# One convolution block with a SwiGLU FFN: the whole convolution input product in seven products, with banks continued from values that ScalarE writes, and late ada rows summed by adding DMAs

## The chip, the core and the metric

One core of a Trainium2 chip runs the kernel. The metric is the device time of one execution in microseconds (us). The engines are TensorE (PE), VectorE (DVE), ScalarE (ACT), GpSimd (POOL) and SyncE (SP); PEld is the loading of weights into PE. Each has its own list of instructions, which it runs in that order; they wait for one another by semaphores. SP issues most loads; POOL issues the stores, and DMAs that add.

## What is computed

One layer over 1024 tokens of width 1024, in fp32: a short gated convolution along the 64 columns of the token grid, then a SwiGLU FFN, each with a modulated RMSNorm ahead and a gated residual behind.

```python
sh1, sc1, g1, sh2, sc2, g2 = jnp.split(jax.nn.silu(c) @ ada_w + ada_b, 6, axis=-1)
h = rmsnorm(x, norm1_g) * (1 + sc1) + sh1
gate_b, gate_c, hv = jnp.split(h @ conv_w_in, 3, axis=-1)
u = gate_c * hv
conv = w[0] * left(u) + w[1] * u + w[2] * right(u)    # within rows of 64 tokens
x = x + g1 * ((gate_b * conv) @ conv_w_out)
h = rmsnorm(x, norm2_g) * (1 + sc2) + sh2
x = x + g2 * ((silu(h @ w_gate) * (h @ w_up)) @ w_out)
out = rmsnorm(x, final_g)
```

The six ada vectors come from one row times a 1024 x 6144 matrix: a sum over rows of weights, each multiplied by one number.

## The kernel before

Every fp32 product is done as three products of rounded parts (TERMS: high x high, high x low, low x high); a high part is a cast on ACT (split at L83, or L254), the low part a subtraction on DVE (L74). A matmul takes 128 x 128 of weights against 512 tokens and adds into one of 8 PSUM banks of 128x512.

The input product h @ conv_w_in has 24 tiles of 128 output columns (8 channel tiles ct for each of j = 0, 1, 2: gate_b, gate_c, hv). Two channel tiles, 0 and 1, are done directly: term0 (L286) runs over the k tiles as soon as each is normalised, in six banks, first for the tokens 0 to 511, later for the others (gated0 and mixed0 take the result). The other six channel tiles are nine pairs in Strassen-Winograd form, class Pair and its subclass Mix (L356): two column tiles by two token halves by two halves of k make seven products P1 to P7 of 12 matmuls each in place of eight. S1 to S4 are sums of the quarters of h, made by operands; weights() makes sums of weight quarters. A pair's products go into three banks X, Y, Z; P1, P6 and P7 are copied out by ACT (L368, L370, L373), and P2, P4, P5, P3 are finished by DVE (c11, c21, c22, c12). in_turn sets the order: products of one pair alternate with those of the one before it and with those of the next.

The ada vectors of the first norm are needed at the start and summed there by class Ada (L148 on ACT, L150 and L152 on DVE). Eight later pieces (two for g1, four for the second norm, two for g2) are loaded between Mixes and FFN products and summed by Ada too: sixteen rows per piece by DVE, or eight, in place. row() then makes high and low parts of the sum and adds over the partitions by two matmuls with a column of ones (L180), then writes a row to DRAM.

Up to the second token half, the order on SP, DVE, ACT and PE is that of the code, written by hand (in_order). Behind it a scheduler sets the order by the code's order as a priority, with tc.issue_after holding ada rows and loads back. The y stage (L670) multiplies the convolution's output by conv_w_out, one tile of 128 tokens at a time; the tiles of x1 go through residual and transposes (L643) to the FFN, which begins at 372.6 us (X_f, Y_f, Z_f at L356; zP at L1034) and fills the rest.

## Time and profile before

| | us |
|---|---|
| median of 3 runs | 1007.99 (1005.8 to 1008.48) |
| the profiled execution | 1006.5 |
| its span | 1004.7 |
| first direct products | 17.7 |
| first products of the y stage | 271.1 |
| first FFN product | 372.6 |

A page gives each engine's busy time and its share of the span, the chain of work that ended last, and groups of instructions by line, engine, operation and tile with busy time, mean duration of one and the idle time before them. In windows, each column is the busy time in a stretch. By stage, the columns being the stretch, PE, PEld, DVE, ACT and POOL busy, the granted clock of PE, the DMA share and GB/s:

```profile
0.00:25.00 25.00, 13.92 (x64) 12.14 (x65) 15.55 (x36) 18.12 (x36) 6.56 (x19) 0.87 1.01 310
75.00:271.00 196.00, 195.45 (x862) 160.00 (x861) 170.51 (x242) 79.64 (x125) 7.62 (x15) 1.00 0.48 144
372.00:1004.00 632.00, 625.26 (x2791) 518.18 (x2789) 435.45 (x630) 259.31 (x414) 47.59 (x82) 1.00 0.45 149
```

### The profile page before, as it was taken

The page shows a single profiled execution, that of the slowest core. Times are in us where ns is not written, and L with a number is a line of the kernel's source. Part 1 is how long each engine was busy: PE and PEld are TensorE (multiplying, and loading weights), DVE is VectorE, ACT ScalarE, POOL GpSimd, SP SyncE. Part 2 cuts the span into 40 slices and gives each one's busy share as a digit, 9 for nine tenths or more (in the row PEclk, how much of TensorE's full clock was granted, in tenths as well). Part 3 has the DMA queues.
Part 4 walks back from the last instruction along what each step waited for, and adds up shares of the span by engine and source line. Part 5 has one row for each costly group of instructions (what it writes and reads, how often), then busy time and mean ns, then how long its engine had stood idle before and what let it go on. Part 6 is the DMA issues. An engine that isn't in the chain of part 4 may idle for free.

```text
span 1004.7 us, 12134 instructions
## 1 busy us (share of the span) xinstructions
PE 983.9 (98%) x4428; PEld 814.1 (81%) x4428; DVE 728.0 (72%) x1087; ACT 446.8 (44%) x722; POOL 83.5 (8%) x153
## 2 busy tenths in 40 slices
PE   5999999999999999999999999999999999999997
PEld 4888888887888878888888888888888888888886
DVE  6879898887935789687666566566566745778875
ACT  7684433333525566233333333333334352534553
POOL 2010000000001110110110110110100110000000
PEclk8999999999999999999999999999999999999999
DMA  9921456343785232364432332332315954577533
GB/s 310 354 70 57 131 149 206 116 148 119 249 232 169 102 108 84 110 205 136 130 115 71 126 110 80 121 107 87 111 45 199 379 210 148 187 254 275 186 128 142
DMA packets 137388, 157.38 MB, mean 157 GB/s; under 512 B 6724, under 2 KB 100016, under 8 KB 137328
## 3 DMA queue, kind: packets, MB, share of 16 engines
q1 hardware_dynamic: 126944, 124.27, 39.4%
q0 software_dynamic: 9152, 29.16, 8.0%
q10 hardware_dynamic: 1232, 3.18, 0.8%
q8 instruction: 34, 0.56, 0.2%
q14 instruction: 26, 0.21, 0.1%
HBM read 123.80 MB, written 32.78 MB: 156 GB/s over the span
## 4 chain that ended last, share of the span: by engine, by line
PE 90%; DVE 4%; DMA 3%; issue 1%; SPq 1%; ACT 0%; POOL 0%; ACTq 0%; DVEq 0%; POOLq 0%
PE X_f L356 23%; PE zP L1034 20%; PE Z_f L356 12%; PE X_m L356 8%; PE y L670 8%; PE Y_f L356 6%; PE u L286 6%; PE Z_m L356 4%; PE Y_m L356 2%; DMA ada_w<-in_ada_w_dram 1%; DMA w0r<-in_conv_w_in_dram 1%; PE x1T L643 1%; DVE BP_f L74 1%; DMA wr_m<-in_conv_w_in_dram 1%; DVE ada_acc L152 1%
## 5 line engine op out<-in xcount | busy, mean ns | idle before, releaser
L74 DVE TENSOR_TENSOR BP_f<-wr_f,BP_f 128x512 fp32r<-128x512 f32 x154 | 104.7, 687 | 60.7 <-ACT BP_f L83 59.0
L83 ACT CAST BP_f<-wr_f 128x512 fp32r<-128x512 f32 x154 | 94.0, 621 | 84.8 <-PE Z_f L356 51.6
L1034 PE MATMUL zP<-w3l_P,a3h_P 128*128 128x512 f32 (+1 forms) x319 | 121.8, 382 | 0.0
L1034 PE MATMUL zP<-w3h_P,a3l_P 128*128 128x512 f32 (+1 forms) x319 | 121.7, 382 | 0.0
L1034 PE MATMUL zP<-w3h_P,a3h_P 128*128 128x512 f32 (+1 forms) x319 | 120.4, 382 | 0.6 <-DVE bot L80 0.6
L1034 PEld LDWEIGHTS zP<-w3h_P,a3h_P 128*128 128x128 f32 x319 | 59.9, 188 | 12.3 <-DVE bot L80 0.8
L1034 PEld LDWEIGHTS zP<-w3l_P,a3h_P 128*128 128x128 f32 x319 | 60.0, 188 | 11.7
L1034 PEld LDWEIGHTS zP<-w3h_P,a3l_P 128*128 128x128 f32 x319 | 60.0, 188 | 11.6
L74 DVE TENSOR_TENSOR a3l_P<-a3l_P,a3h_P 128x1024 fp32r<-128x1024 f32 (+1 forms) x42 | 47.4, 1135 | 26.9 <-ACT a3h_P L889 26.9
L83 ACT CAST BP_m<-wr_m 128x512 fp32r<-128x512 f32 x63 | 37.8, 622 | 58.9 <-DVE wr_m L74 31.8
L152 DVE SCALAR_TENSOR_TENSOR ada_acc<-ada_w,cols,ada_acc 128x512 f32<-128x512 f32 (+1 forms) x88 | 61.3, 709 | 1.6 <-ACT ada_acc L148 0.5
L356 PE MATMUL X_f<-A11h,BP_f 128*128 128x512 f32 x176 | 57.7, 390 | 0.0
L356 PE MATMUL X_f<-AS3h,BP_f 128*128 128x512 f32 x176 | 57.6, 389 | 0.0
L356 PE MATMUL X_f<-AS2h,BP_f 128*128 128x512 f32 x176 | 57.6, 389 | 0.0
L356 PE MATMUL X_f<-A22h,BP_f 128*128 128x512 f32 x176 | 57.6, 389 | 0.0
L356 PE MATMUL Z_f<-AS4h,BP_f 128*128 128x512 f32 x176 | 57.6, 389 | 0.0
L356 PE MATMUL Y_f<-A12h,BP_f 128*128 128x512 f32 x176 | 57.5, 389 | 0.0
L356 PE MATMUL Z_f<-AS1h,BP_f 128*128 128x512 f32 x176 | 57.4, 389 | 0.0
L74 DVE TENSOR_TENSOR BP_m<-wr_m,BP_m 128x512 fp32r<-128x512 f32 x63 | 42.3, 686 | 14.4 <-ACT BP_m L83 13.9
L670 PE MATMUL y<-woh,vh_t 128*128 128x512 f32 x128 | 50.4, 394 | 0.0
L670 PE MATMUL y<-woh,vl_t 128*128 128x512 f32 x128 | 49.9, 390 | 0.0
L670 PE MATMUL y<-wol,vh_t 128*128 128x512 f32 x128 | 49.9, 390 | 0.0
(287 smaller groups left out, 2239.3 us busy)
## 6 DMA issues: line engine op xcount, KB each, us to landing
wr_f<-in_ffn_w_in_dram SPq DMA_DIRECT2D x44, 512.0 KB, 3.9
ada_w<-in_ada_w_dram SPq DMA_DIRECT2D x64, 256.0 KB, 5.9
w_P<-in_ffn_w_out_dram SPq DMA_DIRECT2D x30, 512.0 KB, 5.6
a3l_P<-ad_S SPq DMA_DIRECT2D x20, 512.0 KB, 6.2
wr_m<-in_conv_w_in_dram SPq DMA_DIRECT2D x18, 512.0 KB, 5.5
ad<-a POOLq DMA_DIRECT2D x33, 256.0 KB, 2.6
ada_w<-in_ada_w_dram SPq DMA_DIRECT2D x16, 512.0 KB, 3.9
a3l_P<-ad SPq DMA_DIRECT2D x15, 512.0 KB, 3.7
```

Of the source, the lines that this page charges most:

```text
L74: return nc.vector.tensor_tensor(o, a, b, op=ALU.subtract)
L83: nc.scalar.copy(hi, raw)
L152: nc.vector.scalar_tensor_tensor(acc, self.rows[k], by, acc, op0=ALU.mult, op1=ALU.add)
L286: nc.tensor.matmul(ps0[ct, j, h], lhsT=w0[k][wi][:, j, ct * P:(ct + 1) * P], rhs=h_of(k, h)[hi], start=(k == 0 and i == 0), stop=(k == KD ...
L356: mm = nc.tensor.matmul(ps, lhsT=w[:, wi, 2 * kp + kk, :], rhs=A[aname, kp][hi][:, kk, :], start=(first and kp == 0 and kk == 0 and i == 0 ...
L643: nc.tensor.transpose(ps2[:, i * P:(i + 1) * P], xn[:, k * P:(k + 1) * P], ident)
L670: mm = nc.tensor.matmul(ys[t][n], lhsT=vt[t][vi][:, k, :], rhs=wo[k][wi][:, n * H:(n + 1) * H], start=(k == 0 and i == 0), stop=(k == KD - ...
L1034: mm = nc.tensor.matmul((zs[t] if to is None else to)[:, cols], lhsT=a[ai][:, k % 2, t * P:(t + 1) * P], rhs=w[wi][:, k % 2, cols], start= ...
```

## The change

All 24 column tiles are now done in seven products, as twelve pairs (PAIRS): pair (i, j) is channel tiles i and i + 4 of j. P1 and P2, which need only the first token half, are done at the start: for seven pairs (EARLY) by term0, k tile by k tile, and for five more by class First, four k tiles at a time. P1 is copied to SBUF between (save_p1, L325). The other five products are class Mixes, two pairs at a time in one bank each, in the order P5, P6, P7, P4, P3. After P5, ACT copies the bank to z5 and writes the saved P1 into the bank (L429, L430); P6 goes on adding to it, DVE takes v = bank + z5, P7 goes on; after P4, ACT writes v into the bank (L444) and P3 goes on. Direct products, class Mix and mixed0 go.

For the eight later pieces, class AdaRow loads rows as before; ACT multiplies each in place (L186); POOL's DMAs with accum_op add them (L188, L191): three of 512 KB and one of 256 KB a piece, each on the destination of the one before. In the convolution their tiles are of the pool t_s, which u, cv, xT and the operands use as well. Rows of a piece are no longer held back by issue_after. In the startup, ada pieces have one column tile for k = 0 to 3; weights come as 128x896 (before 128x768) in two DMAs. The y stage begins with three tiles of the first four k's (before two, six k's).

```diff
+    class AdaRow:
+        def __init__(self, j0, nj, d0, w, tile):
+            self.j0, self.d0, self.w = j0, d0, w
+            self.name = f"ada{j0}_{d0}"
+            for k0 in range(0, KD, 2):
+                raw = tile(f"{self.name}_w{k0}", [P, 2, nj, w])
+                for j in range(nj):
+                    nc.sync.dma_start(raw[:, :, j, :], aw[:, k0:k0 + 2, j0 + j, d0:d0 + w])
+                for i in range(2):
+                    nc.scalar.mul(raw[:, i], raw[:, i], cs[:, k0 + i:k0 + i + 1])
+                if k0:
+                    nc.gpsimd.dma_start(both, raw, accum_op=ALU.add)
+                else:
+                    both = raw
+            nc.gpsimd.dma_start(both[:, 0], both[:, 1], accum_op=ALU.add)
+            self.acc = [both[:, 0]]
...
+    PAIRS = [(0, 2), (0, 1), (1, 2), (1, 1), (0, 0), (2, 2), (2, 1), (1, 0), (3, 2), (3, 1), (2, 0), (3, 0)]
+    EARLY = PAIRS[:7]
+    place = {(i, j): 3 * j - 2 + i if j else 0 for i, j in EARLY}
...
     def load0(k):
-        w0raw[k] = t_wraw(f"w0r_{k}", [P, 3, C0 * P])
-        nc.sync.dma_start(w0raw[k], conv_w_in[k * P:(k + 1) * P, :].rearrange("p (j n) -> p j n", j=3)[:, :, :C0 * P])
+        w0raw[k] = t_wraw(f"w0r_{k}", [P, 7, P])
+        rows = conv_w_in[k * P:(k + 1) * P, :]
+        nc.sync.dma_start(w0raw[k][:, 1:, :].rearrange("p (j i) n -> p j (i n)", j=2),
+                          rows.rearrange("p (j n) -> p j n", j=3)[:, 1:, :3 * P])
+        nc.sync.dma_start(w0raw[k][:, 0, :], rows[:, :P])
...
+    def term0(k, pair, terms=range(3)):
+        if pair not in xbank:
+            xbank[pair] = bank("x%d_%d" % pair)
+        for i in terms:
+            wi, hi = TERMS[i]
+            nc.tensor.matmul(xbank[pair], lhsT=w0[k][wi][:, place[pair], :], rhs=h_of(k, 0)[hi],
+                             start=(k == 0 and i == 0), stop=(k == KD - 1 and i == 2), skip_group_check=True)
...
+    def save_p1(pair):
+        n = PAIRS.index(pair)
+        if n % 2 == 0:
+            saved[n // 2] = t_s(f"p1_{n // 2}", [P, 2, H])
+        saved[pair] = saved[n // 2][:, n % 2, :]
+        nc.scalar.copy(saved[pair], xbank[pair])
...
+    def first_done(pair):
+        (i, j), ps = pair, xbank.pop(pair)
+        if j == 2:
+            mixed[i, 0] = t_s(f"u{i}_0", [P, 2, H])
+            nc.scalar.copy(mixed[i, 0][:, 0, :], ps)
+        elif j == 1:
+            mul(mixed[i, 0][:, 0, :], ps, mixed[i, 0][:, 0, :])
+        else:
+            if i % 2 == 0:
+                gate11[-1 - i] = t4(f"gate11_{i}", [P, 2, H])
+            gate11[i] = gate11[-1 - i // 2 * 2][:, i % 2, :]
+            nc.scalar.copy(gate11[i], ps)
...
+    class First:
+        def __init__(self, pair):
+            (i, j), self.pair = pair, pair
+            self.raw = t_wraw("wf%d_%d" % pair, [P, KD, P])
+            nc.sync.dma_start(self.raw, conv_w_in[:, j * D + i * P:j * D + (i + 1) * P].rearrange("(k p) n -> p k n", p=P))
+        def weights(self, half):
+            self.w = [t_wop("wf%s%d_%d_%d" % ((s, half) + self.pair), [P, KH, P]) for s in "hl"]
+            split(*self.w, self.raw[:, half * KH:(half + 1) * KH, :])
+        def products(self, half):
+            if half == 0:
+                xbank[self.pair] = bank("x%d_%d" % self.pair)
+            for k in range(KH):
+                for i, (wi, hi) in enumerate(TERMS):
+                    nc.tensor.matmul(xbank[self.pair], lhsT=self.w[wi][:, k, :], rhs=h_of(half * KH + k, 0)[hi],
+                                     start=(half == 0 and k == 0 and i == 0), stop=(half == 1 and k == KH - 1 and i == 2),
+                                     skip_group_check=True)
+            if half == 0:
+                save_p1(self.pair)
+            else:
+                first_done(self.pair)
...
+    class Mixes:
+        def __init__(self, n):
+            self.n, self.pairs = n, PAIRS[2 * n:2 * n + 2]
+            self.raw = {}
+            for name, tile, k0 in (("11", 0, 0), ("12", 1, 0), ("22", 1, KH), ("21", 0, KH)):
+                self.raw[name] = t_wraw(f"wr{name}_{n}", [P, 2, KH, P])
+                for a, (i, j) in enumerate(self.pairs):
+                    c = j * D + (i + tile * KH) * P
+                    self.last_load = nc.sync.dma_start(
+                        self.raw[name][:, a],
+                        conv_w_in[k0 * P:(k0 + KH) * P, c:c + P].rearrange("(k p) n -> p k n", p=P)).ins
+            self.w = {}
...
+        def weights(self):
+            b11, b12, b22, b21 = [self.raw[name] for name in ("11", "12", "22", "21")]
+            sub(b11, b12, b11)
+            self.weight("P5", b11)
+            yield
+            sub(b11, b22, b11)
+            self.weight("P6", b11)
+            yield
+            sub(b12, b22, b12)
+            self.weight("P7", b12)
+            yield
+            sub(b21, b21, b11)
+            self.weight("P4", b21)
+            yield
+            self.weight("P3", b22)
+            yield
+        def weight(self, pname, raw):
+            w = self.w[pname] = [t_wop(f"B{pname}{s}_m{self.n}", [P, 2, KH, P]) for s in "hl"]
+            split(*w, raw)
...
+        PLAN = (("P5", "S1"), ("P6", "S2"), ("P7", "S3"), ("P4", "22"), ("P3", "S4"))
+        def products(self):
+            ps = [bank(f"m{self.n}_{a}") for a in range(2)]
+            z5, v = [[t2(f"{name}_{self.n}_{a}") for a in range(2)] for name in ("z5", "v")]
+            for pname, aname in self.PLAN:
+                for a, (i, j) in enumerate(self.pairs):
+                    for k in range(KH):
+                        for n, (wi, hi) in enumerate(TERMS):
+                            mm = nc.tensor.matmul(ps[a], lhsT=self.w[pname][wi][:, a, k, :],
+                                                  rhs=A[aname, k // 2][hi][:, k % 2, :],
+                                                  start=(pname == "P5" and k == 0 and n == 0),
+                                                  stop=(k == KH - 1 and n == 2), skip_group_check=pname != "P5")
+                    self.last_mm = mm.ins
+                    if pname == "P5":
+                        nc.scalar.copy(z5[a], ps[a])
+                        nc.scalar.copy(ps[a], saved[i, j])
+                        if j == 2:
+                            mixed[i, 1] = t_s(f"u{i}_1", [P, 2, H])
+                    elif pname == "P6":
+                        add(v[a], ps[a], z5[a])
+                    elif pname == "P7":
+                        to = mixed[i, 1][:, 1, :]
+                        if j == 2:
+                            add(to, ps[a], z5[a])
+                        else:
+                            add(z5[a], ps[a], z5[a])
+                            mul(to, to, z5[a])
+                    elif pname == "P4":
+                        self.put(mixed[i, 0][:, 1, :], ps[a], j)
+                        nc.scalar.copy(ps[a], v[a])
+                    else:
+                        self.put(mixed[i, 1][:, 0, :], ps[a], j)
+                        self.finish(i, j)
...
+                for m, pair in enumerate(EARLY):
+                    term0(k, pair)
+                    if k == KH - 1:
+                        save_p1(pair)
+                    if m == 2 and k == p.ks[-1]:
+                        r.total()
...
+        for n, pair in enumerate(EARLY):
+            for k in (KD - 2, KD - 1):
+                term0(k, pair)
+            if n < TH:
+                xs[n].scale()
+            elif n < TH + 2:
+                more[n - TH].weights(0)
+            first_done(pair)
         transposed(0)
-        two = [next(mix) for _ in range(2)]
-        term0(KD - 1, 0, cts=(0,))
+        more[0].products(0)
         transposed(1)
-        term0(KD - 1, 0, cts=(1,))
-        gated0(0, 0)
-        transposed(2), transposed(3)
...
+    for m in more:
+        m.weights(1)
+        m.products(1)
+    mixes = Mixes(0)
+    weights = mixes.weights()
+    next(weights)
+    for n in range(3):
+        next(ops)
+        next(weights)
+        if n == 1:
+            for kp in range(2):
+                operand("22", kp, xT[1][kp + 2])
+    next(weights)
...
-    def start_piece(p):
+    def start_piece(p, tile):
         with tc.issue_after(p.last_load):
-            a = Ada(*pieces.pop(0), itertools.repeat(t_wraw))
-        a.sums()
-        pending.append(a)
-    def between_mixes(p):
-        if pending:
-            finish_piece(p)
-        if pieces and (p.j != 2 or p.ct == C0):
-            start_piece(p)
-    in_turn(itertools.chain(two, mix), 9, between_mixes)
+            pending.append(AdaRow(*pieces.pop(0), tile))
+    for n in range(6):
+        mixes.products()
+        if n < 5:
+            mixes = Mixes(n + 1)
+            for _ in mixes.weights():
+                pass
+        while pending:
+            finish_piece()
+        for _ in range((1, 1, 2, 2, 0, 0)[n]):
+            start_piece(mixes, t_s)
...
-    K0 = KD - 2
-    for t in range(2):
+    K0, T0 = KD - 4, 3
+    for t in range(T0):
         vt[t] = v_tile(t, ((0, K0), (K0, KD)))
         y_steps(t, range(K0))
     for t in range(2):
-        vt[t + 2] = v_tile(t + 2, ((0, KD),))
+        if t == 0:
+            vt[T0] = v_tile(T0, ((0, KD),))
+        else:
+            vt[T0 + 1] = v_tile(T0 + 1, ((0, KD),))
```

On DVE, at the start of the first Mixes (m0), the changed order runs, from the u product of pair (3, 1) (the first row, u_0_877), to the first v (rows of operands S1 to S4 and of weights BP.. of m0; wr are raw weight quarters):

```order
L80 TENSOR_TENSOR u_0_877<-x_1_759,u_0_877 128x512
L74 TENSOR_TENSOR AS2l_950<-S_0_832,AS2h_949 128x1024
L74 TENSOR_TENSOR wr_0_931<-wr_0_934,wr_0_931 128x1024
L74 TENSOR_TENSOR S_1_833<-S_1_833,xT_1_98 128x1024
L74 TENSOR_TENSOR xT_1_102<-xT_1_98,xT_1_102 128x1024
L74 TENSOR_TENSOR BP5l_m_945<-wr_0_931,BP5h_m_944 128x1024
L74 TENSOR_TENSOR AS2l_955<-S_1_833,AS2h_954 128x1024
L74 TENSOR_TENSOR wr_0_931<-wr_0_937,wr_0_931 128x1024
```

After four more rows of the same kind it ends:

```order
L74 TENSOR_TENSOR A22l_979<-xT_2_103,A22h_978 128x1024
L74 TENSOR_TENSOR xT_2_99<-xT_2_99,S_0_832 128x1024
L74 TENSOR_TENSOR BP7l_m_975<-wr_0_934,BP7h_m_974 128x1024
L74 TENSOR_TENSOR A22l_983<-xT_3_104,A22h_982 128x1024
L74 TENSOR_TENSOR AS4l_988<-xT_2_99,AS4h_987 128x1024
L74 TENSOR_TENSOR xT_3_100<-xT_3_100,S_1_833 128x1024
L74 TENSOR_TENSOR wr_0_940<-wr_0_940,wr_0_931 128x1024
L77 TENSOR_TENSOR v_0_1012<-m_0_1008,z_0_0_1010 128x512
```

In the kernel before, the same operands stood here, interleaved with finishing rows of other pairs, while the direct products of the second token half ran on PE:

```order
L74 TENSOR_TENSOR AS1l_955<-S_0_951,AS1h_954 128x1024
L74 TENSOR_TENSOR S_0_951<-S_0_951,xT_0_97 128x1024
L74 TENSOR_TENSOR xT_2_99<-xT_2_99,S_0_951 128x1024
L74 TENSOR_TENSOR BP_m_2_1023<-wr_m_2_1_612,BP_m_2_1023 128x512
L74 TENSOR_TENSOR BP_m_2_1026<-wr_m_2_1_612,BP_m_2_1026 128x512
L77 TENSOR_TENSOR S_1_952<-xT_1_102,xT_3_104 128x1024
L74 TENSOR_TENSOR xT_1_102<-xT_1_98,xT_1_102 128x1024
L74 TENSOR_TENSOR AS1l_960<-S_1_952,AS1h_959 128x1024
L74 TENSOR_TENSOR AS2l_983<-S_0_951,AS2h_982 128x1024
L74 TENSOR_TENSOR S_1_952<-S_1_952,xT_1_98 128x1024
```

The sums and subtractions are the same; what stands behind them is new: v_0_1012, a drain of a product's bank, where before only rows of later products followed.

On ACT in the fifth Mixes (m4), between the drains of P5 (L429, L430), the changed order has (ada_768 is a piece for the second norm; a trailing x2 means two such rows):

```order
L186 ACTIVATE ada_512_w_1898<-ada_512_w_1898,cols 128x512 x2
L83 CAST BP3h_m_1857<-wr_4_1831 128x1024
L186 ACTIVATE ada_768_w_1905<-ada_768_w_1905,cols 128x512 x2
L186 ACTIVATE ada_768_w_1910<-ada_768_w_1910,cols 128x512 x2
L186 ACTIVATE ada_768_w_1916<-ada_768_w_1916,cols 128x512 x2
L429 COPY z_4_0_1931<-m_0_1929 128x512
L186 ACTIVATE ada_768_w_1922<-ada_768_w_1922,cols 128x512 x2
L430 COPY m_0_1929<-p_4_738 128x512
L429 COPY z_4_1_1932<-m_1_1930 128x512
L430 COPY m_1_1930<-p_4_738 128x512
```

Before, a Mix late in the convolution had (e_m and u_m are copies of a bank, BP_m a weight's high part, cv a convolution's first product):

```order
L83 CAST BP_m_0_1724<-wr_m_0_0_1642 128x512
L370 COPY e_m_1_1528<-X_m_1_1515 128x512
L83 CAST BP_m_0_1727<-wr_m_0_1_1644 128x512
L83 CAST BP_m_0_1732<-wr_m_0_1_1644 128x512
L373 COPY u_m_1_1638<-X_m_1_1515 128x512
L83 CAST BP_m_0_1735<-wr_m_0_1_1644 128x512
L368 COPY e_m_0_1665<-X_m_0_1652 128x512
L83 CAST BP_m_0_1739<-wr_m_0_0_1642 128x512
L294 ACTIVATE cv_1694<-u_1461,cols_576 128x1024
```

There, casts and copies alternated; now eight products of ada rows stand between casts and the copy and write of a bank.

On POOL the first late piece's DMAs are:

```order
L188 DMA ada_0_w_1195<-ada_0_w_1199 128x1024
L188 DMA ada_0_w_1195<-ada_0_w_1204 128x1024
L188 DMA ada_0_w_1195<-ada_0_w_1209 128x1024
L191 DMA ada_0_w_1195<-ada_0_w_1195 128x512
L205 DMA ada_0_b<-in_ada_b_dram 1x16x32
L209 DMA g_row<-ada_0_b 16x1x32
L188 DMA ada_512_w_1413<-ada_512_w_1417 128x1024
```

In their place before:

```order
L312 DMA vd<-cv_0_693 128x512
L312 DMA vd<-cv_0_732 128x512
L312 DMA vd<-cv_1_966 128x512
L312 DMA vd<-cv_1_975 128x512
L183 DMA ada_0_b<-in_ada_b_dram 1x16x32
L187 DMA g_row<-ada_0_b 16x1x32
L183 DMA ada_512_b<-in_ada_b_dram 1x16x32
```

The first four add into ada_0_w_1195, one behind the other; the row matmuls on PE (L202) wait for the last of them through a cast. Before, POOL issued only stores, and rows of ada_b.

More of the change, by code (lines that the diff above doesn't have):

```diff
@@ L253, in modulate1 @@
         nc.scalar.activation(o, o, AF.Identity, scale=scale1[:, k:k + 1], bias=shift1[:, k:k + 1])
-        nc.scalar.copy(h_of(k, h)[0], o)
+        if h == 0:
+            nc.scalar.copy(h_of(k, h)[0], o)
     def low1(k, h):
@@ L277, in low0 @@
         sub(w0[k][1], w0raw[k], f(w0[k][0]))
-    def term0(k, h, terms=range(3), cts=range(C0)):
-        for ct in cts:
-            for j in JS:
-                if k == 0 and 0 in terms:
-                    ps0[ct, j, h] = bank(f"u{ct}_{j}_{h}")
-                for i in terms:
-                    wi, hi = TERMS[i]
-                    nc.tensor.matmul(ps0[ct, j, h], lhsT=w0[k][wi][:, j, ct * P:(ct + 1) * P], rhs=h_of(k, h)[hi],
-                                     start=(k == 0 and i == 0), stop=(k == KD - 1 and i == 2))
+    def term0(k, pair, terms=range(3)):
[5 more added lines that the diff above has]
+                             start=(k == 0 and i == 0), stop=(k == KD - 1 and i == 2), skip_group_check=True)
@@ L517, in trunk_kernel @@
         for i in range(TH):
-            if i == TH - 1:
-                p.sums(3)
             xs[i].scale()
@@ L524, in trunk_kernel @@
                     xs[i].copies(g)
-        p.sums()
+            if i == TH - 2:
+                p.total()
+        xs[-1].copies(0)
         high0(0)
-        for g in range(2):
-            xs[-1].copies(g)
+        r.sums(4, 1)
+        columns(p)
+        xs[-1].copies(1)
         low0(0)
-        p.total()
-        columns(p)
         while r:
@@ L555, in trunk_kernel @@
         low1(KD - 1, 0)
-        for i in range(TH):
-            xs[i].scale()
-        mix = mixes()
+        more = [First(pair) for pair in PAIRS[7:]]
+        squares(xs)
+        cols2 = columns_of("cols2", 4 * KD, rows2)
+        g2c, cwc = cols2[:, R_G2:R_G2 + KD], cols2[:, R_CW:]
         def transposed(i):
@@ L725, in then @@
             h2_of(t - 1 if t > 2 else 0, xr[t - 1 if t > 2 else 0])
-        y_steps(t, range(KD), 6 if t == 3 else 4, then)
+        y_steps(t, range(K0 if t < T0 else 0, KD), 6 if t < 4 else 4, then)
         if t == 2:
```

162 lines of the change are left out of this document (52 added, 110 removed).

## The prediction

> **What bounds the kernel now.** I read the page first: which engine is full, and which engine the chain that ended last runs through.
>
> ```profile
> span 1004.7 us, 12134 instructions
> ...
> PE 983.9 (98%) x4428; PEld 814.1 (81%) x4428; DVE 728.0 (72%) x1087; ACT 446.8 (44%) x722; POOL 83.5 (8%) x153
> ...
> PE 90%; DVE 4%; DMA 3%; issue 1%; SPq 1%; ACT 0%; POOL 0%; ACTq 0%; DVEq 0%; POOLq 0%
> ```
>
> PE is busy 98% of the span and holds 90% of the chain. So a product that goes saves its time only as long as PE finds the next one ready. How close the other engines are is read from the stage that changes. The windows of 25 us through the convolution's products give, from the left, the busy time of PE, PEld, DVE and ACT, the granted clock and the DMA share:
>
> ```profile
> core 0: us, PE busy (x) PEld busy (x) DVE busy (x) ACT busy (x) POOL busy (x), PEclk, DMA share, GB/s
> 75.00:100.00 25.00, 25.00 (x112) 20.71 (x111) 24.76 (x30) 11.49 (x16) 0.00 (x0) 1.00 0.16 50
> 100.00:125.00 25.00, 25.00 (x112) 20.67 (x112) 20.31 (x31) 10.57 (x17) 1.59 (x3) 1.00 0.44 132
> 125.00:150.00 25.00, 25.00 (x112) 20.45 (x111) 24.02 (x36) 9.54 (x15) 0.98 (x2) 1.00 0.53 157
> 225.00:250.00 25.00, 24.45 (x108) 19.65 (x107) 18.96 (x31) 9.88 (x18) 0.52 (x1) 1.00 0.38 114
> ```
>
> PE is full in nearly every one, but DVE stands at 19.0 to 24.8 us of 25: it is a second engine just behind the bound, covered rather than idle. The waits of PE in the part of the span before the FFN say the same (what waited, for whom, us in total, times, longest):
>
> ```profile
> PE cols_ps L106 <- ACT xT L221: 7.3, 1, 7.3
> PE u L286 <- ACT A11h L254: 2.5, 1, 2.5
> PE u L286 <- DVE A11l L74: 0.7, 1, 0.7
> PE X_m L356 <- ACT u_m L373: 0.6, 1, 0.6
> ```
>
> The first three fall at the start. After them, up to the y stage, PE waits once, 0.6 us. All that this kernel can lose is therefore cover, and the question for each edit is how much cover it leaves.
>
> **What the change saves.** The chain gives the price of a product of four k tiles and three terms, and of the second token half's direct products:
>
> ```profile
> 74.12 32.67 PE u L286 x144
> 106.79 2.72 PE X_m L356 x12
> ```
>
> 12 matmuls take 2.72 us, 0.2267 each. Before, input products for channel tiles 0 and 1 are 288 matmuls and the nine Mix pairs 756, together 1044; after, twelve pairs of seven products of 12 are 1008. The 36 that go are worth 36 x 0.2267 = **8.2 us**. This is certain as busy time of PE. The ada sums that leave DVE (64 in the middle of the kernel) are worth nothing directly, since DVE is not the bound, and they come back on ACT and as DMAs.
>
> **What the change takes away: cover.** Before, a Mix spread its products over three banks, and products of one pair alternated with those of the other two; a bank was drained while PE filled others. Now the five products of a pair share one bank, two pairs alternate, and between two products of one bank stand only the 12 matmuls of the other: 2.72 us. In that time ACT or DVE has to read the bank, and after P5 and P4 ACT has to write it as well. Durations, by line and by shape, for ACT and then DVE (busy, mean ns of one, idle before and its releaser):
>
> ```profile
> L253 ACT ACTIVATE xT<-xT,shift,scale 128x512 f32<-128x512 f32 x16 | 12.6, 811 | 1.0 <-DVE shift L170 1.0
> L274 ACT CAST w0h<-w0r 128x768 fp32r<-128x768 f32 x8 | 6.8, 845 | 6.9 <-DMA w0r<-in_conv_w_in_dram 6.9
> L370 ACT COPY e_m<-X_m 128x512 f32<-128x512 f32 x9 | 5.3, 587 | 12.9 <-PE X_m L356 12.9
> L148 ACT ACTIVATE ada_acc<-ada_w,cols 128x512 f32<-128x512 f32 x4 | 2.8, 718 | 4.6 <-DMA ada_w<-in_ada_w_dram 4.6
> L254 ACT CAST A12h<-xT 128x512 fp32r<-128x512 f32 x4 | 2.5, 621 | 0.1
> L83 ACT CAST AS4h<-xT 128x1024 fp32r<-128x1024 f32 x2 | 2.1, 1055 | 0.8 <-DVE AS3l L74 0.5 <-PE u L286 0.3
> ...
> L74 DVE TENSOR_TENSOR w0l<-w0r,w0h 128x768 fp32r<-128x768 f32 x8 | 7.6, 952 | 0.5 <-ACT w0h L274 0.5
> L77 DVE TENSOR_TENSOR e_m<-Y_m,e_m 128x512 f32<-128x512 f32 x6 | 4.1, 685 | 2.9 <-PE Y_m L356 2.9
> L74 DVE TENSOR_TENSOR AS1l<-S,AS1h 128x1024 fp32r<-128x1024 f32 x2 | 2.5, 1226 | 0.0
> ```
>
> A copy out and a write in are 0.59 + 0.59 = 1.2 us, a DVE sum 0.69: each fits in 2.72 if the engine is free at that moment. What stands ahead of them in program order decides.
>
> *Start, +5 us.* At the end of k = 3 the last of seven copies of P1 sums waits for that k's last matmul; behind it, and ahead of the operand that k = 4 begins with, stand an ada product, a modulation and a cast: 0.59 + 0.72 + 0.81 + 0.62 = 2.7 us with nothing left for PE. Before, no copy from a bank stood there. At k = 5 to 6 the new scale and shift come with 12 matmuls (2.7 us) left; two modulations with casts, the high weights, the low weights and the low operand follow one another: 2 x (0.81 + 0.62) + 0.85 + 0.95 + 0.69 = 5.4, so 2.6 us are open (the weight tile is 128x896 now, which I left at the price of 128x768). Together 5.3; I take 5. Bounds: 0, if the 3.2 us that PE waits there before go in exchange and a little more, to 8.
>
> *Mix 0, +7 us.* On DVE, 18 rows of 128x1024 stand between the u product and v of the first bank. The u product waits for the third of five P2 products. From there to the end of the first P6 are five products, 60 matmuls, 13.6 us; another 2.7 us pass under the other bank's P6 before P7 needs v to be done. DVE needs 0.69 + 18 x 1.226 + 0.69 = 23.4 us, 7.1 more. Before, the same preparation had the 144 direct products of the second half as cover, 32.7 us, and DVE was busy 24.8 of 25 even then. Bounds: 4 to 9 (by how far such rows overlap, and how early DVE can run ahead).
>
> *Mix 4, +8 us.* In the ACT order the cast BP3h waits until the last P5 but one matmul is done; behind it, ahead of the write into the first bank for which P6 waits, stand six ada products, a copy and two more products: 1.06 + 8 x 0.72 + 2 x 0.59 = 8.0 us. No product is left to hide them: the other bank's P5 is over. Bounds: 7 to 14, if loads of those ada rows come late.
>
> *Mixes 1, 2, 3 and 5, +7 us.* The same cast stands ahead of the second bank's pair of copies, with one or two ada products in some: 1.06 + 0.59 + 0.59 + 0.72 = 3.0 against 2.72, and more where ACT comes to it late. I take 1 each, and 3 more in Mix 3, where ada products stand ahead of the first copy too. Bounds 0 to 12.
>
> **The adding DMAs, +30 us.** Before has none, so they are bounded by the nearest transfers of the same queue, and the loads they wait for:
>
> ```profile
> ad<-a POOLq DMA_DIRECT2D x33, 256.0 KB, 2.6
> ...
> ada_w<-in_ada_w_dram SPq DMA_DIRECT2D x16, 512.0 KB, 3.9
> ...
> x1d<-x POOLq DMA_DIRECT2D x8, 512.0 KB, 3.0
> ...
> vd<-cv POOLq DMA_DIRECT2D x6, 512.0 KB, 4.5
> ```
>
> A piece has four steps on one destination, each waiting for the one before: 3 x (3.0 to 4.5) + 2.6 = 11.6 to 16.1 us from its last ada product on. After it come the cast, the low part and two row matmuls that stand in PE's order, with PE blocked until they run. A Mix is 120 matmuls, 27.2 us. One piece in a Mix (the first two) fits; but the next Mix's u and cv tiles take the buffers of its raw rows, so DVE and ACT, too, wait for POOL: I take 3 us each. Two pieces in a Mix (twice) need 23 to 32 us of steps, a first load of 3.9 and 16 ada products of 0.72, 39 to 48 us if nothing overlaps, 12 to 20 over the 27.2. I take 12 each, the lower end, since some of it runs beside stalls counted above. 2 x 3 + 2 x 12 = 30. Bounds: 0 if all of it stays inside the Mixes, 80 if a step takes 9 us (six chains of 3 x 9 + 4.5 are 189 us, against 109 in four Mixes).
>
> The Trainium skill, "Collectives: The Full Stack", section "The bandwidth ceiling: the fold count and why AG ≠ RS ≠ AR", says that a reducing transfer runs at about half the rate of a copy, because it reads two sources through one ring. No run here shows an adding DMA yet; by that rule a step would be nearer to 9 us than to 4.5, which is a rival below.
>
> *Nothing for the rest.* In the y stage three tiles begin early instead of two; the matmuls are the same, and the products hide the new order (0 to 5 us, if the first transposes of x1 come late). In the FFN two pieces go from DVE to ACT and POOL under its products, which fill PE.
>
> **Sum.** -8.2 + 5 + 7 + 8 + 7 + 30 = +48.8 us. On the profiled execution of 1006.5 us that is 1055.3; the median of the runs lies 1.5 us above it, which makes **1057 us**.
>
> **Rivals.**
> - *The queues cost, the adding DMAs don't.* If steps of 3.0 us run beside the loads, 30 becomes 0 to 8: 1008 - 8.2 + 27 + 4 = 1031. For: DMA share is only 0.4 to 0.5 in these windows. Against: row matmuls and buffers tie PE and DVE to the last step. With all queue terms at their lower bounds (11 us) it reaches 1011.
> - *Faster: the cover holds.* In the Mix stage ACT is busy only 10 of 25 us and DVE loses the ada sums. If each bank comes back within the 2.72 us of the other one's product, PE stays full and only the 36 matmuls count: 1008.0 - 8.2 = 1000. It decides at that point alone, 2.72 us per drain, and fails where ACT's eight ada products stand in between. Against it: three of the places above go past it by rows that the order fixes.
> - *Slow sums.* With a step at 9 us the term is 80 instead of 30: 1107. For it only that a sum reads twice; against it, nothing in this trace.
>
> **Chances.** Forecast 0.60 (1038 to 1085), queues alone 0.20 (1011 to 1038), faster 0.10, slow sums 0.10 (1085 to 1130). The range 1012 to 1115 leaves out the faster case and about half of the slow one. A measurement of this kernel can tell about 0.3% (3 us) from no change: faster by more 0.10, within it 0.04 (the low edge of queues alone), slower 0.86.
>
> **What would show it.** Right: PE busy 8 us less while the span grows; PE waits in the m banks for ACT's writes, the longest in Mix 4 at some 8 us; a wait of Mix 0 for DVE's v; row matmuls of ada waiting for a cast behind POOL; an adding DMA of 512 KB landing in 3 to 6 us. Wrong: PE full in windows of the Mix stage (then the faster rival); PE waits of ACT alone, with no row matmul or POOL among releasers (queues alone). The forecast fails first if the adding DMAs land well under 3 us or over 9.

## The result, and the profile after

The changed kernel takes 1103.0 us (median of 4 runs, 1098.0 to 1106.5), the kernel before beside it 1007.2: a ratio of 1.0948, 95% interval 1.09 to 1.0996. It is 95.9 us slower, where the forecast of 1057 us stood 49.8 above the same 1007.2; the time lies inside the stated range, but outside the forecast's own 1038 to 1085, in the case of slow sums, which had a chance of 0.10. The four runs lie 8.5 us apart, and the profiled execution is the one of 1098.0. Its page (the span, busy time and share of each engine, the chain that ended last by engine):

```profile
span 1096.3 us, 12225 instructions
...
PE 1003.8 (92%) x4404; PEld 819.4 (75%) x4404; DVE 691.0 (63%) x975; ACT 500.3 (46%) x787; POOL 108.9 (10%) x183
...
PE 61%; DMA 17%; DVE 8%; issue 7%; ACT 4%; SPq 2%; POOL 1%; POOLq 0%; DVEq 0%; ACTq 0%
```

PE holds 61% of the chain, where it held 90%. Two things are to be read from the second line. PE's idle time is 1096.3 - 1003.8 = 92.5 us; before it was 1004.7 - 983.9 = 20.8, so 71.7 us more. And PE is *busy* for longer, though 36 matmuls of 128x512 are gone: 983.9 - 8.2 = 975.7 us were due, 1003.8 are there, 28.1 us more. 71.7 + 28.1 - 8.2 = 91.6 us is the whole difference of the two spans.

By stage, PE is idle 21.5 us up to the first product of the Mixes (11.8 before, up to the last direct product), 57.8 in the Mixes (0.6) and 13.2 behind them (8.5). What PE waited for in the whole span (us in total, times, longest):

```profile
PE m L423 <- ACT m L430: 15.1, 6, 8.7
PE m L423 <- DVE u L77: 14.1, 3, 6.8
PE ada_ps L202 <- ACT ada_h L83: 11.6, 3, 7.8
PE m L423 <- ACT m L444: 10.8, 3, 7.3
PE cols_ps L106 <- ACT xT L243: 6.8, 1, 6.8
PE x L317 <- ACT A11h L277: 4.6, 1, 4.6
PE m L423 <- DVE v L77: 3.7, 1, 3.7
PE X_f L507 <- ACT e_f L521: 2.9, 1, 2.9
PE x L317 <- DVE A12l L74: 2.7, 1, 2.7
PE x L317 <- ACT A12h L277: 2.6, 1, 2.6
```

Four rows, 51.6 us, stand for the Mixes: ACT's writes of p1 (L430) and v (L444), DVE's sum that drains P7 (L77), and row matmuls of ada (L202). Before, the Mixes had one wait of 0.6 us.

The busy time is read from windows (busy us of PE, PEld, DVE, ACT, POOL with the number of instructions, PE's granted clock, DMA share, GB/s), here of two stretches with a gap:

```profile
170.00:180.00 10.00, 3.22 (x9) 2.31 (x8) 2.52 (x3) 1.33 (x2) 1.11 (x2) 0.69 0.81 188
290.00:300.00 10.00, 5.02 (x12) 3.96 (x13) 1.23 (x1) 4.84 (x9) 1.85 (x3) 0.50 1.04 242
```

In the second row 12 matmuls take 5.02 us in place of 2.72: the clock is at half. Over the whole span PE works 44.2 us at a granted clock of 0.5, in ten stretches; before, 6.8 us in one, at the start. By 0.43 us a matmul against 0.227 half of that time would do at full clock, so the clock costs an estimated 22.1 us here and 3.4 before: 18.7 of the 28.1. The timeline of the Mixes shows why, and is the clearest sight of the ACT queue that the prediction read from the order (start, duration, instruction, idle time ahead of it and who ended it; ACT first, then PE):

```profile
286.75 1.03 ACT L83 CAST BP3h_m<-wr 128x1024 fp32r<-128x1024 f32 x1
287.68 3.78 ACT L186 ACTIVATE ada_w<-ada_w,cols 128x512 f32<-128x512 f32 x6
291.37 0.56 ACT L429 COPY z<-m 128x512 f32<-128x512 f32 x1
293.12 1.33 ACT L186 ACTIVATE ada_w<-ada_w,cols 128x512 f32<-128x512 f32 x2 [1.19 <-DMA ada_w<-in_ada_w_dram]
294.35 0.57 ACT L430 COPY m<-p 128x512 f32<-128x512 f32 x1
...
285.92 0.39 PE L423 MATMUL m<-AS1h,BP5l_m 128*128 128x512 f32 x1
294.98 0.79 PE L423 MATMUL m<-AS2h,BP6h_m 128*128 128x512 f32 x1 [8.67 <-ACT m L430]
295.57 0.63 PE L423 MATMUL m<-AS2l,BP6h_m 128*128 128x512 f32 x1
296.00 0.63 PE L423 MATMUL m<-AS2h,BP6l_m 128*128 128x512 f32 x1
```

This is the fifth Mixes' turn from P5 to P6. Behind the cast, six ada products, a copy, a load awaited for 1.19 us and two more products stand ahead of the write: PE is idle for 8.67 us, and starts again at 0.43 us a matmul instead of 0.227, until about 300.2. The Trainium skill, "TensorE: Matmul & The Clock Gate", section "Part 1: The HAM clock gate (the "warmup" mystery)", says that the clock falls to half after an idle window of some 3.4 us and returns after a busy one; the trace agrees at this gap, with half speed for 5.2 us. The gaps of 2.65 and 2.70 us of this trace's start, shorter than such a window, were followed by half speed too, for 3.4 us each, so a gap need not be that long; three others of 2.5 to 2.9 us, at 311, 326 and 565 us, were not.

The adding DMAs, beside transfers of the same size on POOL's queue (KB each, median us to landing):

```profile
ada_w<-ada_w POOLq DMA_DIRECT2D x24, 512.0 KB, 6.1
...
vd<-cv POOLq DMA_DIRECT2D x8, 512.0 KB, 4.3
x1d<-x POOLq DMA_DIRECT2D x8, 512.0 KB, 3.1
...
ada_w<-ada_w POOLq DMA_DIRECT2D x8, 256.0 KB, 4.8
```

A piece's chain is 3 x 6.1 + 4.8 = 23 us from its first step on. What else hangs on it is seen at the second Mixes, in DVE's timeline and PE's:

```profile
168.37 1.22 DVE L74 TENSOR_TENSOR BP6l_m<-wr,BP6h_m 128x1024 fp32r<-128x1024 f32 x1
176.65 0.69 DVE L77 TENSOR_TENSOR u<-m,z 128x512 f32<-128x512 f32 x1 [7.06 <-DMA ada_w<-ada_w]
...
177.39 0.80 PE L423 MATMUL m<-A22h,BP4h_m 128*128 128x512 f32 x1 [6.78 <-DVE u L77]
```

DVE's sum needs a tile for u; the tile is one of the piece's raw rows and is free only when the adding DMA out of it has landed. DVE stands for 7.06 us, with PE's bank undrained.

### The profile page after: what moved, and what is told of

The parts are those of the page before. It is cut to its first block, busy times and chain, and to the rows that moved or that the text cites. A ratio compares the mean times of both kernels' runs of the same rounds, so it can differ in the third digit from the quotient of the medians.

```text
span 1096.3 us, 12225 instructions
## 1 busy us (share of the span) xinstructions
PE 1003.8 (92%) x4404; PEld 819.4 (75%) x4404; DVE 691.0 (63%) x975; ACT 500.3 (46%) x787; POOL 108.9 (10%) x183
## 4 chain that ended last, share of the span: by engine, by line
PE 61%; DMA 17%; DVE 8%; issue 7%; ACT 4%; SPq 2%; POOL 1%; POOLq 0%; DVEq 0%; ACTq 0%
PE zP L1140 19%; PE X_f L507 16%; PE Z_f L507 8%; DMA ada_w<-ada_w 8%; PE y L772 6%; PE m L423 4%; PE Y_f L507 4%; DMA ada_w<-in_ada_w_dram 3%; PE x L317 1%; DVE BP_f L74 1%; DMA vl_t<-vd 1%; DMA w0r<-in_conv_w_in_dram 1%; SPq L140 1%; PE x L358 1%; ACT xT L275 1%
## 5 line engine op out<-in xcount | busy, mean ns | idle before, releaser
L186 ACT ACTIVATE ada_w<-ada_w,cols 128x512 f32<-128x512 f32 x64 | 42.8, 715 | 39.6 <-DMA ada_w<-in_ada_w_dram 38.1
L507 PE MATMUL X_f<-AS3h,BP_f 128*128 128x512 f32 x176 | 57.8, 390 | 2.9 <-ACT e_f L521 2.9
L772 PE MATMUL y<-wol,vh_t 128*128 128x512 f32 x128 | 49.8, 389 | 0.0
L995 ACT CAST a3h_P<-a3l_P 128x1024 fp32r<-128x1024 f32 (+1 forms) x42 | 40.7, 977 | 17.6 <-DMA a3l_P<-ad_S 10.9
L74 DVE TENSOR_TENSOR wr_f<-wr_f,wr_f 128x512 f32<-128x512 f32 x66 | 45.3, 690 | 4.2 <-DMA wr_f<-in_ffn_w_in_dram 2.7
```

Of the source, the lines that this page charges most:

```text
L74: return nc.vector.tensor_tensor(o, a, b, op=ALU.subtract)
L186: nc.scalar.mul(raw[:, i], raw[:, i], cs[:, k0 + i:k0 + i + 1])
L507: mm = nc.tensor.matmul(ps, lhsT=w[:, wi, 2 * kp + kk, :], rhs=A[aname, kp][hi][:, kk, :], start=(first and kp == 0 and kk == 0 and i == 0 ...
L772: mm = nc.tensor.matmul(ys[t][n], lhsT=vt[t][vi][:, k, :], rhs=wo[k][wi][:, n * H:(n + 1) * H], start=(k == 0 and i == 0), stop=(k == KD - ...
L995: nc.scalar.copy(hi, f(lo))
```

## The experiments

Theory, when they began: the time goes to ACT's and DVE's queue at the turns of the banks, to the chain of slow adding DMAs and the tiles that it holds, and a part of each gap again to the lowered clock. Rival 1: the shared bank by itself. Rival 2: the adding DMAs alone, whatever the cover. Runs without a range are single ones, each beside the kernel before at 1007.4 to 1007.6 us. "Bare" is the changed kernel with the late pieces cut to two rows; the pieces' vectors are then not the reference's, as in the runs without adds.

**No adds.** In class AdaRow (in before's form of it too, further down):

```diff
-                if k0:
-                    nc.gpsimd.dma_start(both, raw, accum_op=ALU.add)
-                else:
+                if k0 == 0:
                     both = raw
-            nc.gpsimd.dma_start(both[:, 0], both[:, 1], accum_op=ALU.add)
```

> The changed kernel without the adding DMAs (the rows of the late pieces other than the first are loaded and multiplied, but not added). Theory: the chains of adding DMAs and what is tied to them (row matmuls of ada, the tiles that u and cv take over) cost some 35 us of PE's idle time and some 12 us more by the lowered clock after gaps, so 1055 us (1045 to 1070), with the waits of PE at the ada rows under 3 us and ACT's ada products still ahead of the bank writes of the fifth Mixes (8 us). Rival 1 (the shared bank itself: two pairs, one bank each): 1085 or more. Rival 2 (the adding DMAs are all of it): 1020 or less.

1062.4 us: 40.6 less. PE's waits now (the same lines stand three numbers lower):

```profile
PE m L420 <- ACT m L427: 17.6, 6, 9.7
...
PE ada_ps L199 <- ACT ada_h L83: 3.9, 2, 2.5
PE m L420 <- ACT m L441: 3.0, 3, 1.7
```

The waits for u are gone, the waits for the row matmuls fell from 11.6 to 3.9 and those for v's write from 10.8 to 3.0; the writes of p1, behind ada products, are as late as ever. So the adding DMAs cost 41 us by the medians, or 36 by the spans of the two profiles; three waits that hang on their tiles fell by 30 us, and PE's busy time by 6. Both rivals are out of their ranges.

**Bare.** `range(0, KD, 2)` becomes `range(0, 2, 2)` in AdaRow, without the adds.

> The changed kernel with the late pieces cut to their first two rows (loads, products and adds of the others left out). Theory: the 8 us wait behind ada products in the fifth Mixes goes as well, and what stays is the start (6 us), Mix 0 (7 us) and some casts ahead of bank copies: 1030 us (1020 to 1042). Rival 1 (the shared bank): 1075 or more. Rival 2 (adding DMAs alone): the same as without the adds, within 4 us.

1035.2 us: another 27.2 less; the wait for L427 falls from 17.6 to 3.2. That is what ACT's products and the loads they wait for cost, with the lowered clock behind the gaps (PE loses 6.2 us by it, 17.9 without the adds). Still 27.8 us more than the kernel before, which sums its pieces besides.

**DVE sums.** The late pieces by class Ada as before (`a = Ada(*pieces.pop(0), itertools.repeat(tile)); a.sums()`), in the change's places and with AdaRow's row(). A first form without that row() could not be built and has no time; 1045 us (1030 to 1060) had been expected of it.

> The changed kernel, with the late pieces summed by DVE as before, from the same tiles (nothing left out). Theory (what costs is a chain of slow adding DMAs that holds tiles, and ACT's ada products behind loads that wait for these tiles): no chain, no ada products on ACT, 12 us of DVE per piece instead; in the Mixes with two pieces DVE is over-full: 1050 us (1038 to 1062), with PE's waits for DVE's v and u. Rival 1 (the shared bank): 1080 or more. Rival 2 (adding DMAs alone, no cost of the place of the sums): 1036 or less, as without pieces.

1061.4 us, at the upper end. PE's wait for DVE's v rose to 13.7 us. It gains as much as leaving out the adds, with the whole computation done: the chain was dearer than the sums. But the sums aren't free either, 26 us over the bare kernel.

**Before with the adding DMAs.** AdaRow put into the kernel before, called by its start_piece.

> The kernel before, with its late pieces summed by ACT's products and the adding DMAs in place of DVE (nothing left out). Theory: with three banks a pair and one piece in a Mix the cover hides most of it; row matmuls of ada wait a little: 1013 us (1006 to 1025). Rival 1: 1007, within 3. Rival 2 (the adding DMAs cost by themselves, whatever the cover): 1045 or more.

1057.5 us, +50: the theory fell here, and the time lies in rival 2's range. I had put the loss down to the cover that the change takes away; the kernel with its full cover loses as much. Its waits, SP's wait ahead of the loads of ada rows (L199), and ACT's idle time ahead of the ada products (the last row: busy, mean ns, idle before and its releaser):

```profile
PE X_m L378 <- ACT e_m L392: 21.0, 6, 7.7
PE X_m L378 <- ACT u_m L395: 10.9, 3, 6.8
...
SPq L199 <- DMA ada_w<-ada_w: 86.9, 12, 11.1
...
L201 ACT ACTIVATE ada_w<-ada_w,cols 128x512 f32<-128x512 f32 x64 | 43.7, 717 | 75.1 <-DMA ada_w<-in_ada_w_dram 72.2 <-DVE sa L77 2.7
```

ACT stands 72 us for loads of ada rows, ahead of the copies for which PE waits: a load needs a tile that an adding DMA still holds, and SP waits 86.9 us for such tiles. That the adds merely slow the loads down is not what the trace shows: a load lands 5.8 us after its issue here, 5.5 in the next run, which has no adds. One thing differs from the change besides cover: the rows lie in the pool of raw weights here, which has 5 buffers, not in t_s with its 32. Whether the kernel before would lose as much with more buffers wasn't tried.

**Before with ACT's products, no adds.** The edit of the first experiment in that kernel.

> The kernel before with ACT's ada products, but without the adding DMAs (rows of the late pieces other than the first are loaded and multiplied, not added; with the adds it took 1057.5 us). Theory: what costs is that a tile is held until its adding DMA has landed, so that the next rows load late and ACT's products, which wait for the loads, stand ahead of the bank copies. Without adds the tiles come free at once: 1015 us (1007 to 1025). Rival (ACT's products are in the way by themselves): 1040 or more.

```profile
L201 ACT ACTIVATE ada_w<-ada_w,cols 128x512 f32<-128x512 f32 x64 | 44.0, 719 | 28.6 <-DMA ada_w<-in_ada_w_dram 27.0 <-DVE BP_f L74 1.4
```

1011.2 us. The same products in ACT's queue cost next to nothing here, though DVE has lost its sums; the adds, by the tiles they hold, cost 46, and ACT's wait for the loads falls from 72 to 27 us. So cover hides ACT's products (in the changed kernel they and their loads cost 27) but, with these buffers, not the chain (46 with the cover, 41 without).

**Two banks a pair.** P1's sum is written into the bank of P6, P7 and P4 ahead of time, P5 has its own, and v is written into that for P3:

```diff
-            ps = [bank(f"m{self.n}_{a}") for a in range(2)]
+            xs, zs = [[bank(f"{name}{self.n}_{a}") for a in range(2)] for name in "mz"]
...
+            for a, pair in enumerate(self.pairs):
+                nc.scalar.copy(xs[a], saved[pair])
...
+                    ps = (zs if pname in ("P5", "P3") else xs)[a]
...
                     elif pname == "P6":
-                        add(v[a], ps[a], z5[a])
+                        add(v[a], ps, z5[a])
+                        nc.scalar.copy(zs[a], v[a])
```

In this form no matmul has begun the bank of P6 when ACT writes to it; so the adding-on of P1's sums is not that of the reference, while the instructions timed are the same.

> The changed kernel with two banks for a pair: P1's sum is written into the bank of P6, P7, P4 ahead of time, P5 has a bank of its own, and v is written into that for P3; no product waits for a write by ACT right after it (nothing left out, adding DMAs as in the change). Theory: PE's waits for these writes (25.9 us) go, but ACT still stands behind loads that wait for adding DMAs, and z5 and the u copies come late in their place: 1085 us (1070 to 1098). Rival 1 (the shared bank is the cost): 1065 or less. Rival 3 (the wait only changes its name): 1099 to 1105.

> The changed kernel with the late pieces cut to their first two rows (1035.2 us so) and two banks for a pair. Theory: without ada products ahead, ACT's writes cost PE only 5.4 us, and these go: 1029 us (1026 to 1032). Rival 1 (the shared bank is the cost also without pieces): 1015 or less. Rival 3 (no gain, drains by DVE are late instead): 1034 or more.

1095.7 us with the adding DMAs, 1030.6 bare: 7.3 and 4.6 less. With the adds the waits move from ACT's writes to DVE's sums:

```profile
PE m L426 <- DVE z L77: 16.3, 3, 9.6
PE m L426 <- DVE v L77: 12.6, 4, 6.7
PE m L426 <- DVE u L77: 8.6, 2, 6.4
```

So the shared bank is worth some 5 us by the bare kernels, single runs both; 7.3 is less than the four runs of the change lie apart. Rival 1 is out.

**The start, bare.** The last three copies of P1 stand behind the first operand of k = 4; k = 6 of all pairs ahead of k = 7; the low operand of k = 6 ahead of the low weights of k = 7 (`low1(KD - 2, 0)` above `low0(KD - 1)`).

> The changed kernel with the late pieces cut to their first two rows (1035.2 us so), and in the start the last three copies of P1 behind the first operand of k = 4, the k = 6 products of all seven pairs ahead of those of k = 7, and the low operand of k = 6 ahead of the low weights of k = 7. Theory: the waits of 2.6 and 2.7 us go: 1030 us (1028 to 1033). Rival (Mix 0 is held by DVE anyway, so the time is lost there instead): 1034 to 1036.

1034.0 us, 1.3 less: the rival's time. The 2.6 us wait is down to 0.6 and that of 2.7 us to 1.2, and the first Mixes start 5.5 us earlier (106.7 against 112.2 us), but the last product of the Mixes comes only 1.2 earlier (296.3 against 297.5). The waits of the first Mixes are as long as they were, so the rival's reason isn't shown. The clock is where the 4.3 us between go: the gap of 3.7 us ahead of P7 is followed by 5.9 us of work at half clock (3.4 in the bare run), and a gap of 2.8 us at 288 us by 6.1 (none behind the 2.2 at the same place there). (5.9 + 6.1 - 3.4) / 2 = 4.3. The same gap thus costs more in one run than in another, and the start's order may be worth more than the 1.3 us show: PE is idle 3.4 us less over the span.

**One piece behind each Mix.** `(1, 1, 2, 2, 0, 0)` becomes one each, the last finished ahead of the y stage.

> The changed kernel with one late piece behind each Mix (1, 1, 1, 1, 1, 1 in place of 1, 1, 2, 2), nothing left out. Theory: three steps of 6.1 us and one of 4.8 (23 us) fit in a Mix of 27 us once, not twice; the waits at ada rows and the longest waits for ACT's writes in the fourth and fifth Mixes go: 1075 us (1065 to 1085). Rival (a piece costs the same wherever it stands): 1095 to 1107.

1092.3 us: 11 less where 28 were expected, between the theory's range and the rival's. That two pieces overfill a Mix was at most a part of it; the waits changed place:

```profile
PE m L423 <- ACT m L444: 21.9, 4, 15.3
PE m L423 <- DVE u L77: 11.0, 2, 6.2
```

The wait of 15.3 us stands in the last Mixes, where the change has no piece: ACT's write of v stands behind the cast of a sum for which it waits 9.7 us. What even places gain without that wait isn't shown.

**Adds by POOL.** `nc.gpsimd.tensor_tensor(both, both, raw, op=ALU.add)` in place of each adding DMA.

> The changed kernel with the late rows added by POOL's own arithmetic on the same tiles in place of the adding DMAs (nothing left out). Theory: the chain is what costs, whoever adds: a POOL add of 128x1024 takes at least the 2.8 us of its 128x1024 product at the end of the kernel, so a piece is 3 x 2.8 + 1.4 = 10 us or more against 23, and the time lies between that without adds (1062) and the change (1103): 1072 us (1064 to 1085). Rival (it is ACT's products alone): 1095 or more. Rival (POOL's adds slow DVE down): 1090 or more with DVE's rows of 128x1024 longer than 1.23 us.

1082.1 us, in the range. A piece's chain is 3 x 2.7 + 1.6 = 9.7 us (2722 ns by the first row below, 1553 for the last step), but DVE pays for it: its sums of raw weights, 1222 ns each in the changed kernel, take 1473.

```profile
L188 POOL TENSOR_TENSOR ada_w<-ada_w,ada_w 128x1024 f32<-128x1024 f32 x24 | 65.3, 2722 | 145.6 <-ACT ada_w L186 145.0
...
L74 DVE TENSOR_TENSOR wr<-wr,wr 128x1024 f32<-128x1024 f32 x24 | 35.3, 1473 | 11.2 <-DMA wr<-in_conv_w_in_dram 11.0
```

**All of it together.** DVE's sums, one piece behind each Mix, two banks (with a matmul of 0.23 us that begins the bank of P6 ahead of ACT's write), the start's order. In the second kernel the sixth piece is started and finished among the first y tiles, and the first scale and shift stand ahead of DVE's next sums.

> The changed kernel with everything that the runs point to, nothing left out: late pieces summed by DVE, one behind each Mix; two banks for a pair (a matmul of its own begins the bank of P6, 12 of them, 2.7 us); the start's order of copies and low operands. Theory: 1061.4 with DVE's sums in the change's places, less 5 for the second bank, less 1 to 5 for the start, less some 12 for the even places: 1040 us (1030 to 1050), still above the kernel before since Mix 0's operands and DVE's drains stay. Rival (DVE over-full in every Mix): 1055 or more. Rival (the cover was all): 1005 or less.

> As the combined kernel (1039.4 us), but the sixth late piece is loaded and summed during the first tiles of the y stage, and its row matmuls stand behind the second tile instead of ahead of the stage; in the start, the first scale and shift stand ahead of DVE's sums of the next piece. Nothing is left out. Theory: the wait of 14.5 us at that row and the 7 us behind it go, 1 to 2 us at the start: 1017 us (1012 to 1024), 1% slower than the kernel before, since the start (first product at 24 us, not 17.7) and the preparation of the first Mixes stay. Rival (the sums hold up the residuals of the y stage instead): 1026 or more. Rival (with all of it the 36 products show): 1004 or less.

1039.4 us, then 1021.2 (4 runs, 1020.9 to 1022.0), a ratio to the kernel before of 1.0144 (1.0127 to 1.0161). In the first, one wait of 14.5 us at the last piece's row matmul stood ahead of the y stage; in the second it is gone:

```profile
span 1019.5 us, 12154 instructions
...
PE 988.1 (97%) x4416; PEld 813.4 (80%) x4416; DVE 729.6 (72%) x1039; ACT 459.9 (45%) x723; POOL 80.6 (8%) x151
```

82 of the 96 us are won back, and the change still doesn't pay. PE is idle 31.4 us (20.8 before) and busy 988.1, 9.7 more than the 975.7 + 2.7 of the 12 added matmuls; the clock, at half for 14.2 us of work where it was for 6.8, is 3.7 of that. No version beat the kernel before.

## Why the prediction came out as it did

The sign and most of the places were right, the size was half: +49.8 against +95.9. That the time lies in the range is in part luck: it came out near the 1107 us of a rival whose reason, a step of 9 us, isn't borne out, because terms too small by other reasons add up to as much.

- *Saved, 8.2 us.* The instructions are gone, but PE's busy time rose. **The step that failed first** is that PE's busy time was taken as the number of matmuls times 0.2267. The sum lacked a term for the 28.1 us of other busy time: some 18.7 of it is the lowered clock after gaps. The view of before had that: the matmuls at 21 to 25 us of its trace lie 0.43 us apart. The other 9.4 us aren't explained by it. 12 more matmuls of 128x1 for the ada pieces of the start are a small part, and so is the way busy time is counted: a matmul ahead of a gap counts the 0.39 us of its record, one in a run the 0.227 to the next start. The rest stays open. In the other runs the excess of busy time was 22.4 us with 41.7 of added idle time (no adds; 14.5 by the clock), 10.6 with 26.3 (bare; 2.8), 14.8 with 36.3 (before with adds; 12.3), 1.4 with 3.3 (its products alone; none). So the clock adds up to a third to the idle time, and at times nothing.
- *Start, +5.* The two waits are there as worked out, 2.6 and 2.7 (2.7 and 2.6 predicted). But PE is idle 9.7 us longer up to the Mixes, and each of the two is followed by 3.4 us at half clock, which costs 1.7: the first product waits 4.6 where it waited 2.5, and several waits of 1 us were in no term. Taking the two away gained 1.3 in time and 3.4 in idle time. So 5 is low by the trace, and high by the time of the bare run.
- *Mix 0, +7.* The sum fits, 6.7, but by luck. DVE's v, of which all 7 were expected (4 to 9), cost 3.7; a write by ACT with 1.2 and the weights of P5 with 1.1 and 0.7 make up the rest, and none of them was in the term. Then come 5.8 us of work at half clock.
- *Mix 4, +8.* Right: 8.67, by the very rows named.
- *Other Mixes, +7.* L430 outside these two places is 15.1 - 8.7 - 1.2 = 5.2. But with the loads for which they wait, ACT's products cost 27.2 us in all (from the runs with and without), where the last two terms allowed some 15: the loads were taken as being in time, and the clock again was left out.
- *Adding DMAs, +30.* The mechanism is right, the term mis-sized: 40.6 by leaving them out, clock included. All four steps were counted from a piece's last product; at the second Mixes two of them, at 163.2 and 169.4 us, started ahead of it (173.4). Steps take 6.1 and 4.8 us, above the nearest rows used (3.0 to 4.5 and 2.6) and below the 9 of the rival. By the Trainium skill's rule of half rate for a reducing transfer ("Collectives: The Full Stack", "The bandwidth ceiling: the fold count and why AG ≠ RS ≠ AR"), which that page measured on rings of several ranks and not on an add inside one core, a step should take twice a copy's time; against the copies of this trace, stores on the same queue, it is 6.1 / 3.1 = 2.0 or 6.1 / 4.3 = 1.4. The reason given, two pieces in a Mix, is at most a part: one piece in each gained 11. And cover alone did not decide, since the kernel before, though with fewer buffers for the rows, loses 46 us to the same adds.
- *y stage and FFN, 0.* From the y stage's start to the end it took 5.5 us more, idle time of PE in the main: the FFN has a new wait of 2.9 us at ACT's copy.
- *Rivals.* Faster was wrong for the reason given, ACT's products at the turn of a bank. Queues alone would have been the kernel without adds, 1062.4 (1031 predicted). Slow sums, 1107, came nearest, but not for its reason: a step takes 6.1 us, not the 9 on which it rested, and its term is 40.6, not 80.

Idle time was thus forecast at 57 us (48.8 + 8.2) of 71.7, and PE's longer busy time at none of 28.1, 18.7 of them the clock.

What isn't settled: how much of the products' 27.2 us is the products and how much their loads, since no run separates them in the changed kernel; and whether the last version's 14.8 us over the kernel before (by the spans: 10.6 of idle time, 9.7 of longer busy time and 2.7 of added matmuls, less the 8.2 saved) can be got below zero by a better start and earlier loads for the y stage.

## What to carry to other kernels

Where PE is 98% busy, price a change by its gaps first: what it frees is its matmuls times 0.227 us, and a gap of several us can be paid again in part, since PE starts at half clock behind it: here six gaps of 3.7 to 8.7 us in the Mixes, 38.8 us in all, were followed by 28.3 us of work at half clock, which costs 14 more. Look for whatever waits on a DMA inside a queue that also turns banks around: an adding DMA holds its tile for 6 us, and through the tile it held loads, ACT's products, DVE's sums and PE. A sum on a busy engine (DVE, 0.75 us a row, 1061.4 us) was cheaper than the same sum taken off it as a chain of DMAs (1103.0).

## What the runs showed of the hardware that I had not expected

- PE's clock after a gap: 5.2 us at 0.43 us a matmul after 8.67 us of idleness, and 3.4 us at half clock after gaps of only 2.65 and 2.70. The same gap of 3.7 us was followed by 3.4, 5.8 or 5.9 us of work at half clock in three runs (bare, the change, the start's order).
- An adding DMA from SBUF to SBUF, 512 KB, lands in 6.1 us (4.5 to 9.4), a 256 KB one in 4.8: half the bytes, four fifths of the time.
- POOL's adds of 128x1024 (2.72 us each) lengthen DVE's rows that run beside them: sums of raw weights by 21% in the mean, from 1222 to 1473 ns.
